# Later places for the attention splits, scores and values in the order of weight units of a one-core decoder layer

## The chip, the core and the metric

The kernel runs on one NeuronCore of a Trainium2 chip. The metric is device time in microseconds (us) of one execution of the whole layer, with all weights read from HBM. Five engines work side by side, each through its own queue in order: TensorE (PE; its weight loads are shown as PEld), VectorE (DVE), ScalarE (ACT), GpSimd (POOL) and SyncE (SP). In this kernel SP does nothing but start DMAs of weights, and POOL, once its constants are made, little but start the DMAs of the attention.

## The reference, cut to what matters

One decoder layer on x of 256 rows (positions) and 1024 columns, in float32:

```python
proj  = x @ W_in                      # q | k | v | B | C | h | gate_attn | gate_conv
y_att = attention(rope(q), rope(k), v) @ W_att      # 8 heads of 64, causal over one block of 256
y_cnv = (B * causal_dwconv3(C * h)) @ W_cnv
mix   = (sigmoid(g_att) * y_att + sigmoid(g_cnv) * y_cnv) @ W_o
x     = LayerNorm(alpha * x + mix)
u     = causal_dwconv3(x @ W_up);  f = (silu(u_gate) * u_val) @ W_down
x     = LayerNorm(alpha * x + f)
```

With 256 positions there is one key block only, so the block selection of the full reference falls away: each query attends to the earlier keys, by plain softmax. The biases of the gates are `b_gate`.

## The kernel before

**Weights and units.** TensorE multiplies in a 32-bit format that keeps fewer bits than float32. So each operand is split in two parts: the rounded value ("high") and what is left ("low"), and a product takes three passes: high by high, high by low, low by high. The host packs all weights in the order of use into 63 chunks of up to 1 MB, with two units in most chunks (134 units in all). SP fetches chunks into three buffers (`raw`). For each unit ScalarE writes the high part (`wh`, line 215) and VectorE the low part (`wl`, line 216); nine units of each have a place in SBUF. The call `ahead(u)` (line 329) puts the splits of all units up to u+4 into the queues before the matmuls of unit u.

**Stages.** Units 0 to 23 are the q, k and v columns. Units 24 to 35 are the columns of the short convolution: two units each of h, C and B for the first half of its channels, then the same for the second half. Each takes 24 matmuls (lines 312 to 314). Units 36 to 51 are the sixteen gate units, 16 matmuls each (lines 322 and 324). From unit 52 on come the output weights of attention and convolution (bank `y`), then W_o, W_up and W_down. PE's order after unit 51 isn't touched by the change.

**What sets the order.** The whole program is written out by hand in one order, from which each engine's queue follows. Between the units stands other work: `at(u, f)` notes that f is to be put into the queues behind the matmuls of unit u, and `run(u)` does so. The steps of the attention are set by a table of such numbers, with `C0` = 24. Heads go in pairs p = 0 to 3:

- `rope` and `qk_turn` (line 371), behind unit 24: q and k, which stand by rows, are transposed. VectorE turns 32 by 32 squares (line 357), eight DMAs on POOL's queue write them to DRAM (`qk_home`, line 360), and when all have landed one DMA reads them back as columns (`qk_turned`, line 363).
- `qk_hl(p)` (line 376): the two splits of the turned queries and keys of pair p, one on ScalarE and one on VectorE, into `qkT`.
- `scores(p)` (line 384): 12 matmuls into two banks `s`. `masked(p)` (line 395): on VectorE, scale, mask and row maximum. `exps(p)`: four Exp on ScalarE (line 411), of the sums also.
- `normalize(p)` and `probs_turn(p)` (lines 415 and 423): on VectorE the reciprocal, four products and the squares; then on POOL's queue four DMAs to DRAM (`p_home`), a wait for them, and one DMA back (`sm`).
- `probs_hl(p)` (line 430): the two splits of the turned probabilities into `vpt` (ScalarE, then VectorE). `attend(p)` (line 435): 6 matmuls into a bank `av`. `attend_hl(p)` (line 444): four splits into `aT`.

Beside these stand `conv1`, `conv2` and `conv3` of each half of the convolution (lines 551 to 573) behind units 28, 29 and 30 and behind units 34, 35 and 36; and for each gate unit j `gate_sum(j)` (line 595: a copy on ScalarE, a sum on VectorE), which frees the unit's bank, one of four in turn, and `gate(j)` (line 592), the Sigmoid on ScalarE.

The tile `gates` shares its memory (tag b16) with `qkT`, the tile of squares of the probabilities (tag x) with `qk_turned`.

Of the kernel before, what the change touches and what calls it, by code (L numbers as in the profile page):

```python
# [8 lines left out]
F32 = mybir.dt.float32  # L9
# [4 lines left out]
ALU = mybir.AluOpType  # L14

P = 128
S = 256
# [120 lines left out]
def layer_kernel(ctx: ExitStack, tc: tile.TileContext, x, wpack, cpack, ln1_g, ln1_b, ln2_g, ln2_b, out):  # L138
    nc = tc.nc

    cst = ctx.enter_context(tc.tile_pool(name="cst", bufs=1))
    big = ctx.enter_context(tc.tile_pool(name="big", bufs=1))
# [8 lines left out]
    def acc_bank(name):  # L151
        return psum.tile([P, 512], F32, tag="acc", name=name)

    def ps_bank(name):
        return ps_pool.tile([P, 512], F32, tag="ps", name=name)

    def scratch(shape, name, bufs=None, tag="scr"):
        return tmp.tile(shape, F32, tag=tag, name=name, bufs=bufs or 6)
# [102 lines left out]
    def bias_gate(j):  # L261
        return consts[:, 132 + j:133 + j]
# [53 lines left out]
    def unit_cols_wide(u, bank, b):  # L316


        un = units[u]
        nk = un["h"].shape[1]  # L320
        for k in range(nk):
            nc.tensor.matmul(bank, un["h"][:, k, :], b[:, k].rearrange("p a s -> p (a s)"), start=k == 0, stop=False)  # L322
        for k in range(nk):
            nc.tensor.matmul(bank[:, 0:S], un["l"][:, k, :], b[:, k, 0], start=False, stop=k == nk - 1)  # L324
# [4 lines left out]
    def ahead(u):  # L329
        for v in range(cur["u"], u + LA + 1):  # L330
            split(v)
        cur["u"] = max(cur["u"], u + LA + 1)
# [36 lines left out]
    BIG = {}  # L369
# [85 lines left out]
    def at(u, f, *a):  # L455
        after.setdefault(u, []).append((f, a))

    def run(u):
        for f, a in after.pop(u, []):
            f(*a)  # L460
# [9 lines left out]
    C0 = U[(OFF_H, 0)]  # L470
# [1 line left out]
        at(C0, rope, t)  # L472
        at(C0, qk_turn, t)
    for p in range(4):
        at(C0 + 3 + p // 2, qk_hl, p)
    for p in range(4):
        s = C0 + 4 + 3 * p
        at(s, scores, p)
        at(s + 1, masked, p)
        at(s + 2, exps, p)  # L480
        at(s + 3, normalize, p)
        at(s + 3, probs_turn, p)
        s = C0 + 9 + 4 * p
        at(s + 1, probs_hl, p)
        at(s + 3, attend, p)
        at(s + 4, attend_hl, p)


    def x_split(k):
# [85 lines left out]
    for pr in range(2):  # L575
# [3 lines left out]
        for nm, off in (("h", OFF_H), ("c", OFF_C), ("b", OFF_B)):  # L579
            bank = acc_bank(f"{nm}{pr}")  # L580
# [6 lines left out]


    GB = {}
    gates = None  # L590

    def gate(j):
        nc.scalar.activation(gates[:, j % 8, j // 8, :], GB.pop(("s", j)), AF.Sigmoid, bias=bias_gate(j))

    def gate_sum(j):
# [6 lines left out]
    for j in range(16):  # L602
        at(U[("g", 0)] + max(j, 1), gate_sum, j)
        at(U[("g", 0)] + max(j + 1, 2), gate, j)
    for j in range(16):
        u = U[("g", 0)] + j
        ahead(u)
        GB[j] = acc_bank(f"g{j}")
        unit_cols_wide(u, GB[j], xT)
        if gates is None:  # L610
            gates = big.tile([P, 8, 2, S], F32, tag="b16", name="gates")
        run(u)
    run(U[("g", 0)] + 16)
    assert not after, list(after)
# [9 lines left out]

    def mix(i, bank):
        t = scratch([P, 2, S], f"m{i}")
        nc.vector.tensor_tensor(t, gates[:, i], bank.rearrange("p (a t) -> p a t", a=2), op=ALU.mult)
        nc.vector.tensor_tensor(t[:, 0], t[:, 0], t[:, 1], op=ALU.add)
        M[i] = t[:, 0]

# [3 lines left out]
    for half in range(2):  # L634
        for e in range(2):
            ua, uc = U[("ao", half)] + e, U[("co", half)] + e
            for n in range(2):
                i = half * 4 + e * 2 + n
                if i > 1:
                    mix_hl(i - 2)  # L640
                ahead(uc + n - 1)
                bank = ps_bank(f"y{i}")
                unit_cols(uc, bank[:, 256:512], yT[:, 0], yT[:, 1], n * P)
                unit_cols(ua, bank[:, 0:256], BIG["aT"][:, 0], BIG["aT"][:, 1], n * P)
                mix(i, bank)
# [199 lines left out]
    for c in range(1, NP // 2):  # L845
        for e in range(2):
            i = 2 * c + e
# [123 lines left out]
```

## Time and profile before

| | |
|---|---|
| Time, median of 3 runs | 388.58 us (387.96 to 390.23) |
| Time of the profiled execution | 386.33 us |
| Its span, first to last instruction | 384.5 us |
| Granted TensorE clock, mean | 0.976 |
| PE busy | 360.3 us (94%) |
| DVE busy | 296.2 us (77%) |
| ACT busy | 217.5 us (57%) |

The times are the measured ones; everything else comes from one execution that the hardware profiler recorded. Its own time of 386.33 us is 1.8 us more than its span. Busy time of an engine is a sum over the whole span, and a busy PE also counts matmuls at half clock. What a stage costs is seen in the waits and in the time from one unit to the next. In a row of a timeline stand the start in us, the length in us, the engine, the line, the operation, what it writes and reads, and how many were merged (x2); in brackets stands the idle time of that engine just before, with what ended it. Matmul rows overlap, since they are pipelined: the pace is the distance from start to start.

### The profile page before, as it was taken

To read this page: it belongs to the slowest core of one execution; us is meant where nothing else is said; L and a number is where in the kernel's file an instruction comes from. 1 tells how busy PE (TensorE), PEld (TensorE's weight loads), DVE (VectorE), ACT (ScalarE), POOL (GpSimd) and SP (SyncE) were. 2 spreads that over 40 slices of the span, in tenths; PEclk is the share of its full clock that TensorE was granted. 3 is DMA by queue.
4 is the path that set the end of the run, shared out by engine and by line. 5 is a ranking of instruction groups with operands and counts; after the bars stand their busy time and mean duration, and the time that the engine had idled before them with its cause. 6 is when DMAs were issued, how large, how long until landed. Compare 5 with 4: busy or idle time off the path is not lost.

```text
span 384.5 us, 5500 instructions
## 1 busy us (share of the span) xinstructions
PE 360.3 (94%) x2082; PEld 316.0 (82%) x2082; DVE 296.2 (77%) x500; ACT 217.5 (57%) x360; POOL 24.2 (6%) x55
## 2 busy tenths in 40 slices
PE   8999946999597999999999999999999999999991
PEld 7888945997486889998888888888888888888891
DVE  4886916847858877987975989889696877999784
ACT  4767406625596875563345665767565575766400
POOL 1000400022122000010210000000000000000011
PEclk9999985999989999999999999999999999999997
DMA  7969582472664675558715176274543628562011
GB/s 257 336 237 381 175 293 83 161 248 52 242 201 149 263 281 199 187 196 340 257 73 218 47 282 232 97 300 137 221 175 154 250 86 320 218 220 110 2 55 55
DMA packets 12858, 74.88 MB, mean 195 GB/s; under 512 B 1696, under 2 KB 2336, under 8 KB 5664
## 3 DMA queue, kind: packets, MB, share of 16 engines
q1 hardware_dynamic: 10496, 67.00, 46.7%
q0 software_dynamic: 2192, 7.34, 6.3%
q8 instruction: 16, 0.26, 0.3%
q10 hardware_dynamic: 144, 0.20, 0.1%
q14 instruction: 10, 0.08, 0.1%
HBM read 70.86 MB, written 3.67 MB: 194 GB/s over the span
## 4 chain that ended last, share of the span: by engine, by line
PE 74%; DMA 8%; DVE 7%; ACT 5%; issue 2%; POOL 2%; DVEq 0%; POOLq 0%; ACTq 0%
PE pb L322 19%; PE pb L324 10%; PE d L293 5%; PE d L294 5%; PE d L295 5%; PE g L322 3%; PE q L514 3%; PE k L514 3%; PE v L514 3%; DMA sm<-p_home 2%; DMA p_home<-p_squares 2%; PE y L314 2%; PE y L313 2%; PE y L312 2%; PE o L294 2%
## 5 line engine op out<-in xcount | busy, mean ns | idle before, releaser
L216 DVE TENSOR_TENSOR wl<-raw,wh 128x1024 fp32r<-128x1024 f32 (+1 forms) x70 | 76.8, 1121 | 15.2 <-ACT wh L215 14.7
L198 DVE TENSOR_TENSOR wl<-raw,wh 128x1024 fp32r<-128x1024 f32 x58 | 70.8, 1222 | 20.6 <-ACT wh L193 20.2
L322 PE MATMUL pb<-x1T,wh 128*128 128x512 f32 x320 | 79.8, 391 | 0.0
L193 ACT ACTIVATE wh<-raw 128x1024 fp32r<-128x1024 f32 x58 | 60.8, 1052 | 25.6 <-DMA raw<-in_wpack 25.6
L215 ACT ACTIVATE wh<-raw 128x1024 fp32r<-128x1024 f32 (+1 forms) x70 | 65.7, 971 | 14.7 <-DMA raw<-in_wpack 9.1
L322 PEld LDWEIGHTS pb<-x1T,wh 128*128 128x128 f32 x320 | 58.5, 188 | 11.1
L324 PEld LDWEIGHTS pb<-x1T,wl 128*128 128x128 f32 x320 | 43.7, 190 | 3.1
L324 PE MATMUL pb<-x1T,wl 128*128 128x256 f32 x320 | 44.6, 282 | 0.0
L322 PE MATMUL g<-xT,wh 128*128 128x512 f32 x128 | 32.9, 399 | 4.0 <-DVE gs L599 3.8
L293 PE MATMUL d<-wh,f 128*128 128x512 f32 x80 | 31.3, 391 | 0.0
L294 PE MATMUL d<-wl,f 128*128 128x512 f32 x80 | 31.3, 391 | 0.0
L295 PE MATMUL d<-wh,f 128*128 128x512 f32 x80 | 31.1, 389 | 0.0
L322 PEld LDWEIGHTS g<-xT,wh 128*128 128x128 f32 x128 | 23.2, 190 | 8.6 <-issue 4.3
L734 ACT ACTIVATE fb<-pb 128x512 f32<-128x512 f32 x20 | 11.9, 594 | 16.6 <-PE pb L324 16.1
L752 DVE SCALAR_TENSOR_TENSOR fc<-fb,consts,fc 128x254 f32<-128x254 f32 x40 | 19.3, 483 | 1.4
L324 PEld LDWEIGHTS g<-xT,wl 128*128 128x128 f32 x128 | 18.3, 199 | 1.4
L750 DVE SCALAR_TENSOR_TENSOR fc<-fb,consts,fc 128x255 f32<-128x255 f32 x40 | 19.1, 478 | 0.0
L744 ACT ACTIVATE fc<-fb,consts 128x256 f32<-128x256 f32 x40 | 18.0, 498 | 1.3 <-DVE fb L738 1.3
L324 PE MATMUL g<-xT,wl 128*128 128x256 f32 x128 | 18.6, 290 | 0.0
L295 PEld LDWEIGHTS d<-wh,f 128*128 128x128 f32 x80 | 15.0, 188 | 3.2
L293 PEld LDWEIGHTS d<-wh,f 128*128 128x128 f32 x80 | 15.1, 189 | 2.7
L294 PEld LDWEIGHTS d<-wl,f 128*128 128x128 f32 x80 | 15.1, 189 | 2.6
(181 smaller groups left out, 685.9 us busy)
## 6 DMA issues: line engine op xcount, KB each, us to landing
raw<-in_wpack SPq DMA_DIRECT2D x55, 1024.0 KB, 5.2
raw<-in_wpack SPq DMA_DIRECT2D x6, 896.0 KB, 5.8
p_home<-p_squares POOLq DMA_DIRECT2D x16, 96.0 KB, 2.7
sm<-p_home POOLq DMA_DIRECT2D x4, 384.0 KB, 4.9
qk_home<-qk_squares POOLq DMA_DIRECT2D x8, 128.0 KB, 2.9
qk_turned<-qk_home POOLq DMA_DIRECT2D x1, 1024.0 KB, 5.2
xr<-in_x SPq DMA_DIRECT2D x1, 1024.0 KB, 6.8
ln<-in_ln_g POOLq DMA_DIRECT2D x2, 512.0 KB, 5.4
```

What stands on the lines that cost most here:

```text
L193: nc.scalar.activation(units[u]["h"], raw_of(u), AF.Copy)
L198: nc.vector.tensor_tensor(units[u]["l"], raw_of(u), units[u]["h"].bitcast(F32), op=ALU.subtract)
L215: nc.scalar.activation(h, src, AF.Copy)
L216: (eng or nc.vector).tensor_tensor(l, src, h.bitcast(F32), op=ALU.subtract)
L293: nc.tensor.matmul(o, ah, bh, start=start, stop=False)
L294: nc.tensor.matmul(o, ah, bl, start=False, stop=False)
L295: nc.tensor.matmul(o, al, bh, start=False, stop=stop)
L322: nc.tensor.matmul(bank, un["h"][:, k, :], b[:, k].rearrange("p a s -> p (a s)"), start=k == 0, stop=False)
L324: nc.tensor.matmul(bank[:, 0:S], un["l"][:, k, :], b[:, k, 0], start=False, stop=k == nk - 1)
L514: nc.tensor.matmul(banks[m][t], (xl if p == 2 else xh)[:, k, t * P:(t + 1) * P], wl if p == 1 else wh, start=k == 0 and p == 0, stop=k == ...
L750: nc.vector.scalar_tensor_tensor(c[:, 1:S], pb[:, a * S:a * S + S - 1], w_ffn(1, j), c[:, 1:S], op0=ALU.mult, op1=ALU.add)
L752: nc.vector.scalar_tensor_tensor(c[:, 2:S], pb[:, a * S:a * S + S - 2], w_ffn(0, j), c[:, 2:S], op0=ALU.mult, op1=ALU.add)
```

## The change

The numbers of the table become other ones, and the tile `gates` is made where the first sigmoid is issued, not behind the matmuls of the first gate unit. No operation is added or removed by the diff's lines.

```diff
     for p in range(4):
-        at(C0 + 3 + p // 2, qk_hl, p)
-    for p in range(4):
-        s = C0 + 4 + 3 * p
+        at(C0 + 6 + p, qk_hl, p)
+    for p, s in enumerate((C0 + 8, C0 + 10, C0 + 11, C0 + 12)):
         at(s, scores, p)
         at(s + 1, masked, p)
...
         at(s + 3, probs_turn, p)
-        s = C0 + 9 + 4 * p
-        at(s + 1, probs_hl, p)
-        at(s + 3, attend, p)
-        at(s + 4, attend_hl, p)
+        at(C0 + 16 + 3 * p, probs_hl, p)
+        at(C0 + 18 + 3 * p, attend, p)
+        at(C0 + 19 + 3 * p, attend_hl, p)
...
-    gates = None
 
     def gate(j):
+        if "gates" not in BIG:
+            BIG["gates"] = big.tile([P, 8, 2, S], F32, tag="b16", name="gates")
+        gates = BIG["gates"]
```

By units, for the pairs 0, 1, 2 and 3:

| step | behind unit, before | behind unit, now |
|---|---|---|
| `qk_hl` | 27, 27, 28, 28 | 30, 31, 32, 33 |
| `scores` | 28, 31, 34, 37 | 32, 34, 35, 36 |
| `masked` | 29, 32, 35, 38 | 33, 35, 36, 37 |
| `exps` | 30, 33, 36, 39 | 34, 36, 37, 38 |
| `normalize`, `probs_turn` | 31, 34, 37, 40 | 35, 37, 38, 39 |
| `probs_hl` | 34, 38, 42, 46 | 40, 43, 46, 49 |
| `attend` | 36, 40, 44, 48 | 42, 45, 48, 51 |
| `attend_hl` | 37, 41, 45, 49 | 43, 46, 49, 52 |

The first place is ScalarE's queue around the first split of the turned queries and keys. The number in `wh32` is that of the unit; the number behind the underscore only tells tiles apart. Before:

```order
L215 ACTIVATE wh31_575<-raw11_426 128x1024
L215 ACTIVATE qkT_152<-qk_turned_157 128x2x256 x2
L215 ACTIVATE wh32_610<-raw12_463 128x1024
L215 ACTIVATE qkT_152<-qk_turned_157 128x2x256 x2
L553 ACTIVATE ch0_656<-h0_462 128x512
L215 ACTIVATE wh33_661<-raw12_463 128x1024
L563 ACTIVATE ct0_696<-z0_658,consts_147 128x256 x2
```

And now:

```order
L215 ACTIVATE wh31_575<-raw11_426 128x1024
L215 ACTIVATE wh32_606<-raw12_463 128x1024
L551 ACTIVATE ch0_634<-h0_462 128x512
L215 ACTIVATE wh33_639<-raw12_463 128x1024
L561 ACTIVATE ct0_667<-z0_636,consts_147 128x256 x2
L215 ACTIVATE wh34_677<-raw13_545 128x1024
L215 ACTIVATE qkT_152<-qk_turned_157 128x2x256
L215 ACTIVATE yT_154<-ct0_667 128x512
L215 ACTIVATE wh35_710<-raw13_545 128x1024
```

The high parts of units 32, 33 and 34 and two steps of the convolution now stand ahead of the split that needs `qk_turned`; VectorE's queue moves in the same way.

The second place is VectorE's queue where the gate sums of units 36 and 37 (`gs0`, `gs1`) stand. `sm2` is the tile of pair 2, `vpt` that of the values and the split probabilities. Before:

```order
L417 RECIPROCAL st2_956<-st2_956 128x4
L421 TENSOR_SCALAR sm2_957<-sm2_957,st2_956 128x128 x2
L421 TENSOR_SCALAR sm2_957<-sm2_957,st2_956 128x256 x2
L357 STREAM_TRANSPOSE p_squares_774<-sm2_957 128x6x4x32
L599 TENSOR_TENSOR gs0_1059<-g0_976,gs0_1059 128x256
L599 TENSOR_TENSOR gs1_1062<-g1_1012,gs1_1062 128x256
L216 TENSOR_TENSOR wl42_1068<-raw17_866,wh42_1067 128x1024
L216 TENSOR_TENSOR vpt_153<-sm1_827,vpt_153 128x768
```

And now:

```order
L599 TENSOR_TENSOR gs0_1040<-g0_952,gs0_1040 128x256
L599 TENSOR_TENSOR gs1_1043<-g1_1001,gs1_1043 128x256
L216 TENSOR_TENSOR wl42_1049<-raw17_825,wh42_1048 128x1024
L417 RECIPROCAL st2_973<-st2_973 128x4
L421 TENSOR_SCALAR sm2_974<-sm2_974,st2_973 128x128 x2
L421 TENSOR_SCALAR sm2_974<-sm2_974,st2_973 128x256 x2
L357 STREAM_TRANSPOSE p_squares_911<-sm2_974 128x6x4x32
L599 TENSOR_TENSOR gs2_1087<-g2_1052,gs2_1087 128x256
L216 TENSOR_TENSOR wl43_1091<-raw17_825,wh43_1090 128x1024
L417 RECIPROCAL st3_1033<-st3_1033 128x4
```

The split of the probabilities of pair 1 (`vpt` from `sm1`) has left this place for one three units after that of pair 0, and the four turns of the probabilities follow one another at distances of two, one and one units, where they had three.

The third place is POOL's queue, whose order is the same in both, with the waits of each row in brackets. `p_home1` is the DRAM tile of pair 1. As it is now:

```order
L360 DMA p_home0_158<-p_squares_911 32x4x192 x3
L363 DMA sm0_818<-p_home0_158 128x768 [waits DMASW3_49,DMASW4_49,DMASW2_49,DMASW1_49]
L360 DMA p_home1_159<-p_squares_911 32x4x192 [waits DVE_49]
L360 DMA p_home1_159<-p_squares_911 32x4x192
L360 DMA p_home1_159<-p_squares_911 32x4x192 [waits DMASW0_49]
L360 DMA p_home1_159<-p_squares_911 32x4x192
L363 DMA sm1_919<-p_home1_159 128x768 [waits DMASW6_49,DMASW7_49,DMASW1_49,DMASW0_49]
```

The read back of pair 0 (`sm0`) waits for its four writes, and the writes of pair 1 stand behind that read. So POOL takes the turns one after another: what a turn holds up is the time from its first write to the issue of its read, while the landing of that read holds up nothing on POOL. (The DMAs take eight counters in turn; the wait for DMASW0 is for an earlier DMA on the same counter.) Nothing moved here but what lies between the turns on the other engines.

More of the change, by code (lines that the diff above doesn't have):

```diff
@@ L609, in layer_kernel @@
         unit_cols_wide(u, GB[j], xT)
-        if gates is None:
-            gates = big.tile([P, 8, 2, S], F32, tag="b16", name="gates")
         run(u)
@@ L626, in mix @@
         t = scratch([P, 2, S], f"m{i}")
-        nc.vector.tensor_tensor(t, gates[:, i], bank.rearrange("p (a t) -> p a t", a=2), op=ALU.mult)
+        nc.vector.tensor_tensor(t, BIG["gates"][:, i], bank.rearrange("p (a t) -> p a t", a=2), op=ALU.mult)
         nc.vector.tensor_tensor(t[:, 0], t[:, 0], t[:, 1], op=ALU.add)
```

## The prediction

> **What bounds the kernel now.** I read the page first, then PE's waits, then the timelines of the engines between 49 and 147 us, and the windows for the clock. The page, with PE's busy tenths and granted clock in 40 slices of 9.6 us:
>
> ```profile
> span 384.5 us, 5500 instructions
> PE   8999946999597999999999999999999999999991
> PEclk9999985999989999999999999999999999999997
> ```
>
> PE is busy from end to end but for two dips, in the sixth and seventh slice (48 to 67 us) and in the eleventh (96 to 106 us); the clock is low in the first dip and after the second. So PE bounds the kernel, and its holes are what an order can win. All of PE's waits from 37 to 150 us:
>
> ```profile
> PE s L392 <- ACT qkT L215: 8.6, 1, 8.6
> PE g L322 <- DVE gs L599: 3.8, 1, 3.8
> PE av L293 <- ACT vpt L215: 1.1, 1, 1.1
> ```
>
> They all belong to the attention or stand behind it. The timeline of PE around the largest, with starts that give the pace of each kind of work:
>
> ```profile
> 49.36 0.28 PE L312 MATMUL b<-xT,wh 128*128 128x256 f32 x1
> 49.48 0.28 PE L313 MATMUL b<-xT,wh 128*128 128x256 f32 x1
> ...
> 52.12 0.28 PE L314 MATMUL b<-xT,wl 128*128 128x256 f32 x1
> 60.99 0.47 PE L392 MATMUL s<-qkT 64*128 64x128 f32 x2 [8.59 <-ACT qkT L215]
> ```
>
> PE ends unit 28 at 52.12 + 0.28 = 52.40 and stands until 60.99, since `scores(0)` comes next and its operands aren't there. Units 29 to 31, which don't need them, stand behind it. The chain that ended last says what was late:
>
> ```profile
> 47.88 6.60 DMA qk_home<-qk_squares
> 55.06 5.22 DMA qk_turned<-qk_home
> ```
>
> The turned queries land at 55.06 + 5.22 = 60.3. The clock of the stretches, as windows (us; busy time and count of PE, PEld, DVE, ACT and POOL; PEclk; DMA share; GB/s):
>
> ```profile
> 52.40:55.40 3.00, 0.00 (x0) 0.00 (x0) 0.00 (x0) 0.00 (x0) 0.34 (x1) 1.00 1.01 422
> 55.40:65.60 10.20, 4.36 (x24) 3.95 (x25) 4.46 (x8) 4.65 (x8) 0.24 (x1) 0.50 0.31 112
> 106.60:110.10 3.50, 3.50 (x14) 3.12 (x13) 3.47 (x13) 3.47 (x6) 0.95 (x3) 0.51 0.39 95
> ```
>
> After each long hole the clock is halved for a while: a second loss of about 4.36 / 2 = 2.2 us and 3.50 / 2 = 1.7 us.
>
> **The floor.** What must PE do from 52.40 to the first matmul of `y`, if it never waits?
>
> ```profile
> 73.05 0.95 PE L392 MATMUL s<-qkT 64*128 64x128 f32 x12
> 73.93 0.39 PE L312 MATMUL c<-xT,wh 128*128 128x256 f32 x1
> ...
> 136.71 0.40 PE L293 MATMUL av<-vpt 128*128 128x512 f32 x1
> 137.76 0.63 PE L322 MATMUL g<-xT,wh 128*128 128x512 f32 x2
> ...
> 146.13 0.28 PE L312 MATMUL y<-yT,wh 128*128 128x256 f32 x1
> ```
> ```profile
> 143.50 1.84 PE g L322 x8
> 145.34 0.95 PE g L324 x8
> ```
>
> A unit of the convolution is 24 matmuls at 0.12 us (49.48 - 49.36) = 2.88; seven are left, 20.2. A gate unit is 1.84 + 0.95 = 2.79; sixteen, 44.6. Scores take 73.93 - 73.05 = 0.88, four times, 3.5; the values 137.76 - 136.71 = 1.05, four times, 4.2. Together 72.5: `y` could begin at 124.9 where it begins at 146.1. So 21.2 us is all that this change can win. Behind 146.1 PE's order is the old one, and I count that part at nothing either way: units 52 and up have their splits as far ahead as before.
>
> **Part 1, the first splits stand three units later.** The landing at 60.3 is not made earlier: `rope` and the turn keep their place. But PE now goes on with units 29 to 32, and needs `qkT` only behind unit 32, at 52.4 + 4 x 2.88 = 63.9. ScalarE and VectorE still wait for the landing, with the splits of unit 34 done; PE has work for 52.4 + 6 x 2.88 = 69.7, so the hole of 8.6 and its half clock go, if the landing isn't late. It may be: the two queues now split units 32 and 33 before they wait, which frees a `raw` buffer at about 52.4, and SP fetches a chunk of 1 MB just when the turned queries are read. The DMA engines were full until 55.4 (share 1.01, 422 GB/s). A chunk that takes its turn there costs between nothing and 1 MB / 422 GB/s = 2.5 us; I take 1.5, since the share after 55.4 is only 0.31. The Trainium skill, page "DMA: Bandwidth & Descriptors", section "Issuing engines are not separate DMA queues", says that DMAs of SP and POOL run on the same 16 engines and interleave; by it alone the delay would be near the upper end, and the sum 1 us longer. No run here shows that overlap yet.
>
> **Part 2, VectorE's queue becomes dense.** The steps of four pairs now stand between units 32 and 39, beside the weights, the second half of the convolution and the first gate sums. VectorE begins at the landing, and PE's next hard demand on it is `attend(0)` behind unit 42, which needs the `vpt` split behind unit 40. Rows of VectorE's timeline, each step from its start to the next one's:
>
> ```profile
> 60.97 1.29 DVE L216 TENSOR_TENSOR qkT<-qk_turned,qkT 128x512 fp32r<-128x512 f32 x2 [11.63 <-ACT qkT L215]
> ...
> 64.79 0.68 DVE L556 TENSOR_TENSOR z<-c,ch 128x512 f32<-128x512 f32 x1
> ...
> 66.53 0.28 DVE L400 CUSTOM_DVE_ANT_0 sm<-s,mask 128x128 f32<-128x128 f32 x1
> ...
> 67.83 1.92 DVE L566 SCALAR_TENSOR_TENSOR ct<-z,consts,ct 128x256 f32<-128x256 f32 x4
> 69.66 1.22 DVE L216 TENSOR_TENSOR wl<-raw,wh 128x1024 fp32r<-128x1024 f32 x1
> 70.80 0.68 DVE L572 TENSOR_TENSOR ct<-b,ct 128x512 f32<-128x512 f32 x1
> 72.18 0.69 DVE L216 TENSOR_TENSOR yT<-ct,yT 128x512 fp32r<-128x512 f32 x1 [0.70 <-ACT yT L215]
> ...
> 74.27 0.17 DVE L417 RECIPROCAL st<-st 128x4 f32<-128x4 f32 x1
> ...
> 76.42 1.19 DVE L216 TENSOR_TENSOR wl<-raw,wh 128x1024 fp32r<-128x1024 f32 x1
> ```
> ```profile
> L599 DVE TENSOR_TENSOR gs<-g,gs 128x256 f32<-128x256 f32 x16 | 6.6, 419 | 6.5 <-ACT gs L598 6.4
> L216 DVE TENSOR_TENSOR vpt<-sm,vpt 128x768 fp32r<-128x768 f32 x4 | 3.8, 953 | 5.6 <-ACT vpt L215 5.6
> ```
>
> In that stretch stand ten low parts (units 35 to 44) at 70.80 - 69.66 = 1.14, 11.4; four `qkT` splits at 1.29 / 2, 2.6; `z` 0.68; four masks at 67.83 - 66.53 = 1.30, 5.2; the taps 69.66 - 67.83 = 1.83; twice the last step of the convolution at 0.68 + 0.69, 2.7; four times reciprocal, products and squares at 76.42 - 74.27 = 2.15, 8.6; five gate sums at 0.42, 2.1; one `vpt` split, 0.95. Sum 36.0 us, so from 60.97 VectorE is there at 97.0 at the earliest. PE without a wait reaches `attend(0)` at 52.4 + 7 x 2.88 + 4 x 0.88 + 7 x 2.79 = 95.6. The two run level, and each late handoff makes PE wait. Those are: two waits for `yT` of 0.70 (row 72.18), and ScalarE's Exp and Sigmoid with their table loads in between; I take 2.5 us (nothing to 6). With 1.5 from part 1, `attend(0)` is at 101.0.
>
> Before that, unit 40 needs the bank of unit 36, freed by a gate sum that stands behind the third pair's softmax; this is the place of the old wait of 3.8 us, and it will again be short by about 2. It is part of the same lag, not a further term.
>
> **Part 3, ScalarE's table.** All Exp now stand ahead of all Sigmoids; before, a Sigmoid stood between the third and the fourth pair's Exp.
>
> ```profile
> L411 ACT ACT_TABLE_LOAD x2 | 2.6, 1283 | 0.0
> L593 ACT ACT_TABLE_LOAD x2 | 2.6, 1283 | 0.9 <-DVE gs L599 0.9
> ```
>
> Two of the four loads of 1283 ns go. ScalarE is the less loaded engine, so I count this at nothing by itself; it keeps the 2.5 us of handoffs from being more. That `gates` is made later moves no operation: the first Sigmoid stood behind the last scores before and does now.
>
> **Part 4, the round trips of the probabilities.** On POOL:
>
> ```profile
> 76.80 2.19 POOL L360 DMA_DIRECT2D p_home<-p_squares  x4 [21.16 <-DVE p_squares L357]
> 81.60 0.57 POOL L363 DMA_DIRECT2D sm<-p_home  x1 [2.61 <-DMA p_home<-p_squares]
> ...
> 118.64 2.19 POOL L360 DMA_DIRECT2D p_home<-p_squares  x4 [8.28 <-DVE p_squares L357]
> 126.36 0.57 POOL L363 DMA_DIRECT2D sm<-p_home  x1 [5.53 <-DMA p_home<-p_squares]
> ```
> ```profile
> 81.60 6.22 DMA sm<-p_home
> ```
>
> A turn holds POOL for 81.60 + 0.57 - 76.80 = 5.4 to 126.36 + 0.57 - 118.64 = 8.3 us, and its read lands about 6 later. Now four turns queue up: the first is ready when VectorE has done 13.9 us of the list above (2.6 + 1.4 + 5 x 1.14 + 1.3 + 0.7 + 2.15), with the 4 us of lateness at about 78. At 8.3 each the reads are issued by 86, 95, 103 and 111 and land by 92, 101, 109 and 117. They are wanted by ScalarE behind units 40, 43, 46 and 49, that is at about 98, 107, 115 and 124. Hidden, with 6 us to spare; if that cover goes, each us beyond it is one us of PE.
>
> **The sum.** After `attend(0)` at 101.0 come four times 1.05 and nine gate units: 101.0 + 4.2 + 25.1 = 130.3. PE then has waited 130.3 - 124.9 = 5.4 us in two or three holes of 1 to 3 us. The hole of 3.8 us before cost a stretch at half clock, 1.7 us, that of 1.1 none; I take one such stretch: 132.0. The Trainium skill, page "TensorE: Matmul & The Clock Gate", section "Part 1: The HAM clock gate", has the clock halved after an idle window of about 3.4 us, the windows running free. The half stretch from 106.6 to 110.1 agrees; by that rule holes of 2 us would mostly cost nothing, and `y` would begin at 130.3.
>
> So `y` begins 146.1 - 132.0 = 14.1 us earlier. The profiled execution of 386.33 us becomes 372.2; it lies 2.3 under the median of 388.58, from which I subtract the same: **374.5 us**.
>
> **The rivals.** *No engine is late* (17 to 21 us won, 367.4 to 371.6): VectorE's 97.0 is within 1.4 us of PE's 95.6, and if landing and handoffs cost little, only the floor is left. Against it speak the many handoffs between two dense queues. 0.17.
>
> *The turned data come late* (2 to 9.5 us won, 379 to 386.6): the DMA engines, which now also carry weights without a pause, stretch the landing at 60.3 by 5 to 12 us, and every us goes to `attend(0)`. For it speaks the share of 1.01 at 52.4; against it that only one freed chunk can stand in the way. 0.10.
>
> *The wait only moves* (within 0.5%, 1.9 us, which is what a measurement can tell from no change): landing later by 12 us or more, or VectorE's handoffs costing as much. 0.04.
>
> *Slower: the four round trips queue up on POOL.* They lie close now, under a VectorE that never pauses. If a turn holds POOL for x, the fourth lands at 78 + 4x + 6, and `y` follows 132.0 - 124 = 8 us later: 92 + 4x. It decides from x = 13.5, where that is 146; at x = 16 `y` begins at 156, and the time is 398.5. Against it: no turn above took over 8.3, and the four writes of the first were issued in 2.19 us, in part under a running `wl` (row 76.42). The Trainium skill, page "SBUF — State Buffer", section "SBUF: two separate sides", has a rule against this change: while VectorE runs operations that take both port pairs, GpSimd can't write the descriptors of its DMAs. The 2.19 us row doesn't show it. 0.04.
>
> **How the numbers follow.** My forecast, 9.5 to 17 us won, has 0.65. The range takes in the middle of the first rival and the milder half of the second: 369.0 to 381.0. Faster by over 0.5%: 0.65 + 0.17 + 0.10 = 0.92, less 0.01 for what borders on no change: 0.91; within 0.5% 0.05; slower 0.04.
>
> **What would show it.** Right: no wait of PE for `qkT` over 2.5 us, clock near 1.0 from 55 to 65 us; `qk_turned` landed by 63; PE's holes then at unit 40 for `gs` and at `attend(0)` for `vpt`, together 3 to 7 us; two table loads fewer; the four `sm` landed ahead of ScalarE's splits; `y` at 128 to 136. Wrong: ScalarE waiting for `sm`, `qk_turned` after 66, VectorE with gaps between 61 and 100 while PE waits, or a stage behind `y` that takes longer than its 238.4 us (384.5 - 146.1) now.

## The result and the profile after

The changed kernel takes 373.68 us (median of 4 runs, 373.11 to 374.72) beside 388.27 us for the kernel before on the same chip (387.46 to 390.23): a ratio of 0.962, with a 95% interval of 0.9576 to 0.9664. The prediction was 374.5 us, faster. The profiled execution of the changed kernel took 373.11 us, with a mean granted clock of 0.988 (0.976 before).

The page of the changed kernel, with PE's busy tenths and granted clock in slices of 9.3 us:

```profile
span 371.3 us, 5482 instructions
...
PE   8999999989989999999999999999999999999991
...
PEclk9999999998999999999999999999999999999997
```

The deep dips of the sixth, seventh and eleventh slice are gone. Two shallow ones are left, in the ninth and the twelfth, and the clock falls once, to 8 tenths. The span is 384.5 - 371.3 = 13.2 us shorter. Two rows of PE's timeline, the scores of the last pair and the first matmul of `y`:

```profile
80.98 0.58 PE L392 MATMUL s<-qkT 64*128 64x128 f32 x3 [1.82 <-DVE st L400]
...
132.96 0.28 PE L312 MATMUL y<-yT,wh 128*128 128x256 f32 x1
```

`y` begins at 132.96, where it began at 146.13: 13.2 us again, so all of it was won ahead of `y`. PE's waits of the changed kernel from 37 to 150 us (us in total, times, longest):

```profile
PE av L294 <- DVE vpt L216: 1.9, 1, 1.9
PE s L392 <- DVE st L400: 1.8, 1, 1.8
PE g L322 <- DVE gs L599: 0.6, 1, 0.6
PE s L392 <- DVE qkT L216: 0.4, 1, 0.4
PE s L392 <- ACT qkT L215: 0.2, 1, 0.2
```

The wait of 8.6 us for the turned queries has become two waits of 0.6 together. What is left, 4.9 us, is nearly all for VectorE. The windows of the changed kernel: the stretch that ran at half clock before, the one that does now, and all that lies from `y` on.

```profile
55.40:65.60 10.20, 9.60 (x83) 9.13 (x82) 2.52 (x3) 1.89 (x3) 0.58 (x1) 1.00 0.59 232
82.75:86.15 3.40, 3.40 (x12) 2.82 (x11) 3.37 (x12) 0.63 (x4) 0.57 (x1) 0.50 0.26 65
132.95:371.30 238.35, 230.47 (x1290) 201.56 (x1288) 195.69 (x306) 130.41 (x205) 6.09 (x8) 0.99 0.48 177
```

From 55 to 65 us the clock is now full. One stretch of 3.4 us at 0.50 is left, behind the wait of 1.8 us at the last scores. From `y` on it takes 238.35 us; 384.5 - 146.13 = 238.4 before. So all is won ahead of it. Windows from the first matmul of unit 24 (`h`) to the first of `y` part it, of the kernel before:

```profile
37.85:146.13 108.28, 92.96 (x617) 84.26 (x616) 74.81 (x148) 63.48 (x120) 16.18 (x29) 0.94 0.57 197
```

And of the changed kernel:

```profile
37.54:132.96 95.42, 90.44 (x618) 82.29 (x617) 75.21 (x147) 61.08 (x119) 16.23 (x29) 0.98 0.65 226
```

PE stood for 108.28 - 92.96 = 15.3 us and now for 95.42 - 90.44 = 5.0: 10.3 won. Its busy time fell by 92.96 - 90.44 = 2.5, since less of the same work runs at half clock. Together that is the 108.28 - 95.42 = 12.9 us of the distance; the other 0.3 lie ahead of `h` (37.85 to 37.54).

The chain of the changed kernel, where the turned data come from:

```profile
48.12 6.99 DMA qk_home<-qk_squares
...
55.70 7.41 DMA qk_turned<-qk_home
63.13 0.64 ACT qkT L215
```

They land at 55.70 + 7.41 = 63.1, 2.8 us later than before. VectorE's timeline from there: the first and last row of the list that the prediction made, its longest idle time, and the gate sums of units 36 and 37:

```profile
63.79 0.69 DVE L216 TENSOR_TENSOR qkT<-qk_turned,qkT 128x512 fp32r<-128x512 f32 x1 [6.36 <-ACT qkT L215]
...
75.77 0.69 DVE L554 TENSOR_TENSOR z<-c,ch 128x512 f32<-128x512 f32 x1 [1.26 <-ACT ch L551]
...
92.47 0.75 DVE L599 TENSOR_TENSOR gs<-g,gs 128x256 f32<-128x256 f32 x2
...
102.76 0.95 DVE L216 TENSOR_TENSOR vpt<-sm,vpt 128x768 fp32r<-128x768 f32 x1
```

The list runs from 63.79 to 102.76 + 0.95 = 103.71, and it is its last row that PE waits for with the first values (`vpt`, 1.9 us above). The first gate sum begins 92.47 - 63.79 = 28.68 us behind the first split; this distance comes back below. POOL's first and third turn of the probabilities, and ScalarE's table loads and splits of them between 60 and 150 us:

```profile
80.38 2.19 POOL L360 DMA_DIRECT2D p_home<-p_squares  x4 [24.11 <-DVE p_squares L357]
84.97 0.57 POOL L363 DMA_DIRECT2D sm<-p_home  x1 [2.40 <-DMA p_home<-p_squares]
...
97.98 2.26 POOL L360 DMA_DIRECT2D p_home<-p_squares  x4
107.46 0.57 POOL L363 DMA_DIRECT2D sm<-p_home  x1 [7.22 <-DMA p_home<-p_squares]
```
```profile
L215 ACT ACTIVATE vpt<-sm 128x768 fp32r<-128x768 f32 x4 | 3.4, 844 | 0.1
...
L411 ACT ACT_TABLE_LOAD x1 | 1.3, 1283 | 0.0
L593 ACT ACT_TABLE_LOAD x1 | 1.3, 1283 | 0.0
```

A turn holds POOL for 84.97 + 0.57 - 80.38 = 5.2 us at the start and for 107.46 + 0.57 - 97.98 = 10.1 us in the third pair, more than the 8.3 seen before. ScalarE waits 0.1 us in all ahead of its four splits of `vpt`: the turns are hidden. The loads are two instead of four.

### The profile page after: what moved, and what is told of

It is laid out like the page before. It is cut to its first block, busy times and chain, and to the rows that moved or that the text cites. A ratio compares the mean times of both kernels' runs of the same rounds, so it can differ in the third digit from the quotient of the medians.

```text
span 371.3 us, 5482 instructions
## 1 busy us (share of the span) xinstructions
PE 357.4 (96%) x2082; PEld 314.2 (85%) x2082; DVE 296.2 (80%) x500; ACT 214.2 (58%) x358; POOL 24.2 (7%) x55
## 4 chain that ended last, share of the span: by engine, by line
PE 70%; DVE 11%; DMA 9%; ACT 5%; issue 2%; POOL 1%; SPq 1%; DVEq 0%; ACTq 0%; POOLq 0%
PE pb L322 20%; PE pb L324 10%; PE d L293 5%; PE d L294 5%; PE d L295 5%; DMA raw<-in_wpack 5%; PE g L322 4%; DVE wl L216 4%; ACT wh L215 3%; PE g L324 2%; PE y L312 2%; PE y L314 2%; PE y L313 2%; DMA qk_turned<-qk_home 2%; PE o L293 2%
## 5 line engine op out<-in xcount | busy, mean ns | idle before, releaser
L732 ACT ACTIVATE fb<-pb 128x512 f32<-128x512 f32 x20 | 11.8, 592 | 13.3 <-PE pb L324 12.7
```

## The experiments

**The theory** behind the prediction: the hole at the turned queries goes since PE has other units to do there, and what is left of the win is set by VectorE's list from the landing to the first values. **The rivals** tested with it: that the later splits, the later values or the fewer table loads bring the win, and not the later scores; and that something other than VectorE's list (landing, round trips, clock) holds the rest. Ratios are to the kernel before in rounds on one chip, with their 95% intervals; the changed kernel's is 0.962 (0.9576 to 0.9664). The chips differ from experiment to experiment, and the kernel before took 386.79 to 388.27 us on them, so a time of one experiment compares with that of another only to about 1.5 us. The traces of two kernels start a little apart, so stages are compared by the distance from `h` to `y` in the two windows above: 108.28 before, 95.42 after.

### The splits at their old place

```diff
-        at(C0 + 6 + p, qk_hl, p)
+        at(C0 + 3 + p // 2, qk_hl, p)
```

> The changed kernel, with the splits of the turned queries and keys back behind units 27 and 28, and all else at its new place. My theory (the order lets ScalarE and VectorE work on while the turn is under way, and VectorE's queue from the landing to the first values sets the time): PE runs to the end of unit 31 (61 us) and then waits some 2 to 3 us for the weights of unit 32, whose splits now stand behind the landing; VectorE has the low parts of units 32 to 34, z and the taps still to do after the landing, about 6 us more, and the landing is earlier by up to 2.5 us since no chunk is fetched beside it. So the first values 2 to 4 us later than in the changed kernel, y at 135 to 137 us, time 376 to 378 us. Rival (only the place of the scores matters, since it alone made PE wait): y at 133 us, time 373.7 us as in the changed kernel.

Measured: 380.38 us, 0.9835 (0.9776 to 0.9895). By the distance from `h` to `y`, 139.81 - 38.89 = 100.92, that is 5.5 us more than the changed kernel (6.7 by the times), more than the 2 to 4 of the theory; the rival's 373.7 is out. The waits and one window of this kernel:

```profile
ACT qkT L215 <- DMA qk_turned<-qk_home: 19.0, 1, 19.0
...
PE c L312 <- ACT ch L551: 5.5, 1, 5.5
```
```profile
65.75:72.60 6.85, 5.06 (x23) 5.07 (x24) 6.61 (x12) 4.54 (x8) 0.00 (x0) 0.50 0.22 44
```

ScalarE stands for 19.0 us at the split for which the data aren't there. What PE then lacks first isn't, as expected, the weights of unit 32. It is a bank: conv1's copy (line 551), which reads the `h` bank, stands on ScalarE behind that split, and unit 32 needs a bank. PE stands for 5.5 us and then runs 6.85 us at half clock. So the splits must stand later as well; a wait at the head of a queue holds back all that stands behind it.

### The values nearer, and the values later

```diff
-        at(C0 + 16 + 3 * p, probs_hl, p)
-        at(C0 + 18 + 3 * p, attend, p)
-        at(C0 + 19 + 3 * p, attend_hl, p)
+        at(C0 + (14, 17, 19, 21)[p], probs_hl, p)
+        at(C0 + (16, 19, 21, 23)[p], attend, p)
+        at(C0 + (16, 19, 21, 23)[p] + 1, attend_hl, p)
```

> The changed kernel, with the splits of the turned probabilities behind units 38, 41, 43 and 45 (3, 4, 5 and 6 units behind their turns, as far as they stood before the change) and the values two units behind each. My theory (the turns follow one another on POOL, some 10 us each, so the later places of the values are needed): pairs 0 and 1 arrive in time, the reads of pairs 2 and 3 land at about 113 and 122 us and are wanted at about 108 and 116; ScalarE and VectorE stand still for them with weights behind, PE waits 3 to 8 us in all, time 376 to 381 us. Rival (the places of the values are free, only those of the scores count): within 1 us of 373.7.

Measured: 373.05 us, 0.9638 (0.9605 to 0.9671). The theory fell here: one turn was late, by 1.3 us on ScalarE, and PE never waited 3 to 8 us for the values (0.2 in all). The wait moved to unit 40. Two lines of this kernel's waits:

```profile
PE g L322 <- DVE gs L599: 2.2, 1, 2.2
...
ACT vpt L215 <- DMA sm<-p_home: 1.3, 1, 1.3
```

In the second kernel the numbers are (18, 21, 23, 25) for `probs_hl` and (20, 23, 25, 27) for `attend`:

> The changed kernel, with the splits of the turned probabilities behind units 42, 45, 47 and 49 and the values behind 44, 47, 49 and 51. My theory (VectorE is behind by about two units at the first values and catches up after): PE's wait of 1.95 us at the first values goes, the gate units that run instead wait at most 0.5 us for their banks, y at 131 us, time 371.5 to 372.5 us. Rival (VectorE's backlog passes on to the banks of the gate units, so the wait only moves): no change, 373.7 us.

Measured: 373.16 us, 0.9645 (0.9603 to 0.9688), no change that the intervals can tell, as the rival had it. Its wait at unit 40, and the window behind it:

```profile
PE g L322 <- DVE gs L599: 2.2, 1, 2.2
```
```profile
94.60:98.05 3.45, 3.45 (x14) 3.08 (x13) 2.81 (x8) 3.42 (x8) 0.00 (x0) 0.51 0.25 65
```

The wait of 1.9 us for the first values is gone, the one for `gs` has grown from 0.6 to 2.2, and the stretch at half clock (3.45 / 2 = 1.7 us) now lies behind it. From the nearer to the later of these places the time is the same: the values don't carry the gain.

### A chunk of weights held back at the landing

```diff
 def ahead(u):
-        for v in range(cur["u"], u + LA + 1):
+        la = 3 if u == C0 + 5 else 2 if u == C0 + 6 else LA
+        for v in range(cur["u"], u + la + 1):
             split(v)
-        cur["u"] = max(cur["u"], u + LA + 1)
+        cur["u"] = max(cur["u"], u + la + 1)
```

> The changed kernel, with the splits of units 33 and 34 put behind the first split of the turned queries, so that no buffer comes free and no chunk of weights is fetched while the turn is read back. Theory: in the changed kernel the read took 7.4 us, in the old one 5.2, because of that chunk; so here the landing is at 60 to 61.5 us, where it was at 63.1. VectorE's list after the landing grows by two low parts, 2.3 us, so the first gate sums end within 1 us of where they did (93.2), and the time stays within 1 us of the changed kernel's. Rival (the landing itself sets the time): y and the end 2 us earlier. Rival (the longer read has another cause): landing at 63 and the time 2 us longer.

Measured: 374.63 us, 0.9688 (0.9646 to 0.973). The read of `qk_turned` in its trace, and two new waits:

```profile
DMA to landing us min/median/max: 5.6/5.6/5.6
```
```profile
PE c L314 <- DVE wl L216: 0.8, 1, 0.8
...
PE c L312 <- ACT wh L215: 0.5, 1, 0.5
```

The read took 5.6 us beside 7.4 in the changed kernel and 5.2 before. While it ran the DMA engines moved 200 GB/s x 5.6 us = 1.1 MB, in the changed kernel 302 x 7.41 = 2.2 MB: there the chunk of weights flows at the same time. How much of the longer read is the chunk's is less sure, since the kernel with the splits at their old place moved only 186 x 6.59 = 1.2 MB in its read, and that took 6.6 us. Nothing was won: the weights held back came late themselves (0.8 + 0.5 us), and VectorE's first gate sum stood 93.52 - 62.58 = 30.9 us behind its first split, in place of 28.7, which is the two low parts that now stand behind the landing. From `h` the first split came 1.7 us earlier (62.58 - 38.05 = 24.5 beside 63.79 - 37.54 = 26.2) and `y` 0.5 later (134.00 - 38.05 = 95.95): the earlier landing and the longer list just add up.

### The softmax of the first pair one unit later

```diff
-        at(s + 3, normalize, p)
-        at(s + 3, probs_turn, p)
+        at(s + 3 + (p == 0), normalize, p)
+        at(s + 3 + (p == 0), probs_turn, p)
```

> The changed kernel, with the softmax end and the turn of the first pair one unit later, behind unit 36, so that the mask of the second pair comes ahead of them and frees the banks of the last scores 2 us earlier. Theory (the sum of PE's waits is set by how far VectorE's queue has come at the gate sums and the first values, not by each wait): the wait of 1.83 us for the last scores goes, the one for the first gate sum, 0.62 us, grows by about as much, and the time stays within 1 us of the changed kernel's (a stretch at half clock may come or go, 1.7 us). Rival (each wait stands for itself): the time 1.8 us less.

Measured: 374.01 us, 0.9649 (0.9615 to 0.9684). The wait of 1.8 us at the last scores is gone, and the one for `gs` has grown from 0.6 to 3.5. Rows of VectorE's timeline, of its waits and of its windows:

```profile
65.62 0.69 DVE L216 TENSOR_TENSOR qkT<-qk_turned,qkT 128x512 fp32r<-128x512 f32 x1 [7.01 <-ACT qkT L215]
...
94.30 0.75 DVE L599 TENSOR_TENSOR gs<-g,gs 128x256 f32<-128x256 f32 x2
```
```profile
PE g L322 <- DVE gs L599: 3.5, 1, 3.5
```
```profile
94.10:101.00 6.90, 6.23 (x19) 5.30 (x20) 5.69 (x15) 6.45 (x16) 2.38 (x5) 0.51 0.47 184
```

94.30 - 65.62 = 28.68 us, the same as in the changed kernel, although the steps between stand in another order. (It is 28.67 to 28.68 in the two kernels with the values moved and in the next one, too.) So the waits of PE are shares of one lag: the step that is moved out of one wait is paid in the next. All of PE's waits from 37 to 150 us sum to 4.9 us here, and to 5.0 in the changed kernel. `y` begins 135.40 - 39.16 = 96.24 us behind `h`, 0.8 later than there, with 6.9 us at half clock in place of 3.4.

### The last Exp behind the first gates

```diff
-        at(s + 2, exps, p)
+        at(s + 2 + (p == 3), exps, p)
```

> The changed kernel, with the Exp of the last pair one unit later, behind the first two Sigmoids, so that ScalarE loads its tables four times there, as before the change, and not twice: 2.6 us more on ScalarE. Theory (VectorE's queue is the bound and ScalarE only hands over to it): the last softmax end and the third and fourth gate sum come 1 to 3 us later, y 0.5 to 2.5 us later, time 0.5 to 2.5 us more than the changed kernel's 373.7. Rival (ScalarE has room, loads are hidden): within 0.5 us.

Measured: 373.96 us, 0.9646 (0.9615 to 0.9676): the theory fell, and the two loads that this brings back cost nothing that can be measured. One window over the whole stretch:

```profile
60.00:132.80 72.80, 67.02 (x434) 59.08 (x433) 57.81 (x121) 53.86 (x107) 10.98 (x20) 1.00 0.59 209
```

This execution has no half clock at all, and its `y` begins at 132.80, 94.84 us behind `h`, 0.6 less than in the changed kernel with its 1.7 us of lost clock. Its first values wait for a `vpt` split that ends at 102.59 + 0.95 = 103.54, 39.6 us behind its first split at 63.94. So the loads don't make VectorE's list longer (39.9 us in the changed kernel), and the half clock at 83 us of the changed kernel costs little: every wait of VectorE in its list there is for ScalarE, none for PE, so PE would else wait longer for the same row of VectorE.

### The products of the softmax on ScalarE

```diff
-                nc.vector.tensor_scalar(pr[:, j, PCOL[t]], pr[:, j, PCOL[t]], st[:, 12 + i:13 + i], None, op0=ALU.mult)
+                nc.scalar.activation(pr[:, j, PCOL[t]], pr[:, j, PCOL[t]], AF.Copy, scale=st[:, 12 + i:13 + i])
```

> The changed kernel, with the four products of each softmax end on ScalarE in place of VectorE: 4 x 1.0 us off VectorE's queue, some 1.5 to 1.8 us more per pair on ScalarE and two more handovers per pair. Theory (VectorE's queue from the landing to the first gate sums and the first values sets what is left of PE's waits): two of the four ends lie ahead of the gate sum that unit 40 waits for, so that comes 1 to 2 us earlier, the wait of 1.95 us for the first values shrinks to under 1 us, time 1 to 3 us less than the changed kernel's. Rival (the handovers cost what the queue gains): within 1 us, or longer.

Measured: 381.45 us, 0.9839 (0.9806 to 0.9871). The theory of a lighter VectorE fell. The waits:

```profile
DVE p_squares L357 <- ACT sm L421: 6.5, 4, 1.6
...
ACT sm L421 <- DVE st L417: 5.8, 4, 1.4
...
PE g L322 <- DVE gs L599: 3.5, 2, 2.7
PE av L293 <- ACT vpt L215: 2.7, 1, 2.7
```

The products take VectorE 1.01 us a pair, 4 in all. Moved, each pair is handed to ScalarE and back, and VectorE stands 6.5 us for the return alone. Work that is taken from the limiting engine, but that this engine then waits for, doesn't shorten its list.

### The scores spread over the gate units

The old distance of three units between the pairs, but from unit 32 on, so that the hole at the turned queries stays away:

```diff
-    for p, s in enumerate((C0 + 8, C0 + 10, C0 + 11, C0 + 12)):
+    for p, s in enumerate((C0 + 8, C0 + 11, C0 + 14, C0 + 17)):
```

> The changed kernel, with the scores behind units 32, 35, 38 and 41, three apart as before the change (mask, Exp and turn one, two and three units behind each); splits and values of the probabilities stay at the new places. My theory (density of VectorE's queue ahead of the first values is what is left of PE's waits): VectorE has one mask and two softmax ends, 5.6 us, less to do ahead of the first values, so the waits of 1.8, 0.6 and 1.95 us go, at the price of four more table loads on ScalarE; y at 127 to 130 us, time 368 to 371 us. Rival (the close place of the scores is what brought the gain, since Exp and Sigmoid then don't alternate): slower than the changed kernel by 2 us or more.

Measured: 387.64 us, 0.9983 (0.9948 to 1.0019): all of the gain is gone, and the theory, which saw a lighter VectorE, fell clearly. Waits, a row each of ScalarE's and of PE's timeline, and the loads:

```profile
PE av L293 <- ACT vpt L215: 5.7, 3, 2.4
...
ACT vpt L215 <- DMA sm<-p_home: 4.2, 1, 4.2
...
PE g L322 <- DVE gs L599: 3.4, 3, 1.8
...
PE av L294 <- DVE vpt L216: 1.7, 4, 0.6
```
```profile
96.88 0.91 ACT L593 ACTIVATE gates<-gs,consts 128x256 f32<-128x256 f32 x2 [4.81 <-PE s L392]
```
```profile
143.70 0.50 PE L293 MATMUL av<-vpt 128*128 128x512 f32 x1 [1.73 <-ACT vpt L215]
```
```profile
L411 ACT ACT_TABLE_LOAD x3 | 3.8, 1283 | 0.1
L593 ACT ACT_TABLE_LOAD x3 | 3.8, 1283 | 0.0
```

ScalarE has become the late engine. Its first Sigmoid waits 4.81 us for scores, since the gates write over the memory of `qkT`; Exp and Sigmoid take turns, with six loads; and the last pair's turn, begun later, is late: ScalarE waits 4.2 us for it, and PE at 143.70 for ScalarE, right ahead of `y` (145.63). Two kernels take away one of the first two each. In the first the gates are Exp, too, so this kernel leaves out the Sigmoid:

```diff
-        nc.scalar.activation(gates[:, j % 8, j // 8, :], GB.pop(("s", j)), AF.Sigmoid, bias=bias_gate(j))
+        nc.scalar.activation(gates[:, j % 8, j // 8, :], GB.pop(("s", j)), AF.Exp, bias=bias_gate(j))
```

> The kernel with the scores spread over units 32, 35, 38 and 41, with Exp in place of Sigmoid for the gates: the gates are then no gates (that part of the function is changed), but ScalarE does the same count of steps of the same size and never changes its table there. In the spread kernel with Sigmoid, y began at 145.6 us and the time was that of the kernel before. Theory (it was lost to six table loads, 1.28 us each, that stand in the chain copy, gate sum, bank): without them PE's waits in the gate units fall from some 12 to under 5 us, y at 131 to 136 us, time 371 to 377 us. Rival (not the loads but the Exp, masks and softmax ends themselves among the gate units, and the splits of the values right behind them): y at 141 us or later, time over 382 us.

Measured: 382.55 us, 0.9836 (0.9781 to 0.9891). Five of the six loads of that stretch are gone (5 x 1.28 = 6.4 us), and `y` begins 140.38 - 39.65 = 100.73 us behind `h`, where the spread kernel has 145.63 - 38.37 = 107.26: 6.5 less. That is less than the theory's 371 to 377 us would need, so the loads are a part and not the whole. The wait for the memory is still there:

```profile
ACT gates L593 <- PE s L392: 6.1, 1, 6.1
```

In the second the first eight gates have the memory of another tile, that of the rows of q and k (tag rows), so that none of them meets `qkT`:

```diff
-        if "gates" not in BIG:
-            BIG["gates"] = big.tile([P, 8, 2, S], F32, tag="b16", name="gates")
-        gates = BIG["gates"]
-        nc.scalar.activation(gates[:, j % 8, j // 8, :], GB.pop(("s", j)), AF.Sigmoid, bias=bias_gate(j))
+        if j == 0:
+            BIG["gates", 0] = big.tile([P, 8, S], F32, tag="rows", name="gates")
+        if j == 8:
+            BIG["gates", 1] = big.tile([P, 8, 2, S], F32, tag="b16", name="gatesc")[:, :, 0]
+        nc.scalar.activation(BIG["gates", j // 8][:, j % 8], GB.pop(("s", j)), AF.Sigmoid, bias=bias_gate(j))
```

> The spread kernel (scores behind units 32, 35, 38 and 41) with memory for the first eight gates that the turned queries and keys don't use (that of the q and k rows, which are done), and the other eight where all were. Theory (the spread kernel's first Sigmoid stood 4.8 us on ScalarE, 6.1 in the one with Exp, until the scores of the third pair had been read from the shared memory, with the gate sums behind it): that wait goes, PE's wait of 1.75 us for the gate sum of unit 38 too, and y comes 2 to 5 us earlier than at 145.6, time 382 to 386 us; the table loads' share of some 5 us stays. Rival (the wait was slack on ScalarE): time as in the spread kernel, 387.6 us.

Measured: 380.74 us, 0.983 (0.9796 to 0.9864); `y` begins 139.60 - 38.72 = 100.88 us behind `h`, 6.4 less and more than the 2 to 5 of the theory; the rival is out. The longest of PE's waits that remain:

```profile
PE av L293 <- ACT vpt L215: 4.0, 2, 2.4
```

So the spread costs 107.26 - 95.42 = 11.8 us of distance, and 1.7 more behind `y` (240.07 us to the end in place of 238.35), which neither edit wins back. Loads and memory are each shown to cost, but the two gains don't simply add up. In both kernels PE's busy time from `h` to `y` falls too, from 95.10 us to 91.56 and 91.79, since less of it runs at half clock. These some 3.4 us stand in either gain and can be won only once. With both edits about 6.5 + 6.4 - 3.4 = 9.5 us would go, as an estimate; the late turn of the last pair, for which ScalarE still waits 3.7 and 2.2 us in the two kernels, is the third cost. No kernel had both edits.

### The low parts of two units on POOL

```diff
-            split(v)
+            split(v, nc.gpsimd if v in (C0 + 11, C0 + 12) else None)
```

> The changed kernel, with the low parts of units 35 and 36 computed on POOL, which stands idle from 56 to 80 us, in place of VectorE: 2 x 1.14 us less in VectorE's list between the landing and the first values. Theory (that list sets PE's waits): the masks, gate sums and values come 2 us earlier, PE's waits of 1.8, 0.6 and 1.95 us fall to under 2.5 in all, time 1 to 3.5 us less than the changed kernel's 373.7, if POOL takes no more than 5 us for each (no trace here shows such a step; unit 35 is needed at 72 and unit 36 at 76 us, and their high parts are there at 67 and 68). Rival (POOL is slower than that, or VectorE's steps beside it get longer): time as before or more, with PE waiting for the low part of unit 35 or 36.

Measured: 376.17 us, 0.9707 (0.9668 to 0.9745): slower than the changed kernel, and the theory fell. POOL's timeline, and VectorE's beside it:

```profile
67.62 5.23 POOL L216 TENSOR_TENSOR wl<-raw,wh 128x1024 fp32r<-128x1024 f32 x2 [11.05 <-ACT wh L215]
```
```profile
68.09 5.31 DVE L216 TENSOR_TENSOR qkT<-qk_turned,qkT 128x512 fp32r<-128x512 f32 x2 [0.78 <-ACT qkT L215]
```

POOL takes 5.23 us for two low parts. In that time VectorE does two splits of 0.69 each, and they last 5.31. VectorE was to save 2 x 1.14 us and loses 5.31 - 2 x 0.69 = 3.9; its first gate sum stands 95.56 - 64.63 = 30.9 us behind its first split, in place of 28.7. With the later values as well (the numbers of the second kernel above):

> Both: the low parts of units 35 and 36 on POOL, and the splits of the turned probabilities and the values one to two units later as in the kernel with the values behind 44, 47, 49 and 51. Theory (VectorE's list sets the waits, and a first wait for gate sums under 1.6 us starts no stretch at half clock): no wait of PE over 1 us from 65 us on, y at 129 to 131 us, time 369.5 to 371.5 us. Rival (POOL's steps cost what they bring): 373 us or more.

Measured: 374.41 us, 0.9657 (0.9624 to 0.9691). The theory fell here too: PE waits 3.8 us for the last scores, whose masks stand behind the two long splits. Whether a hole under 1.6 us never starts a stretch at half clock, this kernel can't tell, since its one stretch follows that long wait. No kernel was found that beats the changed one by more than a measurement can tell.

## Why the prediction was right, point by point

**Sign, size and mechanism held**: 13.2 us of the profile against 14.1 predicted, 373.68 against 374.5. How near the number came is in part luck. Two terms of the sum were off, and they offset each other. And the profiled execution of the kernel before lies 388.27 - 386.33 = 1.9 us under the median, that of the changed one 0.6, so the medians differ by 14.6 us where the profiles differ by 13.2.

**What bounds the kernel.** The three lines given as all of PE's waits from 37 to 150 us are three of seven: the others, 0.9, 0.5, 0.3 and 0.2 us, are waits for VectorE. The forecast doesn't rest on them, since its floor is counted from PE's work.

**Part 1.** The hole of 8.6 us and its half clock went. The prediction has PE covered until 69.7, which is a step too far: `scores(0)` stands behind unit 32 in PE's queue, so the cover ended at the 63.9 that the text has just before. The two waits for `qkT`, 0.6 us together, are what the landing at 63.1 cost there. The landing was mis-sized: a delay of 1.5 us was taken, between nothing and 2.5, and the read alone took 7.41 - 5.22 = 2.2 more, the writes ahead of it end 0.6 later: 63.1 in place of 61.8, just past the 63 of the text. The kernel that holds the chunk of weights back (5.6 us) points to the chunk as the cause; that one read without a chunk took 6.6 leaves its exact share open. The rule of the Trainium skill that the prediction cited here ("DMA: Bandwidth & Descriptors", section "Issuing engines are not separate DMA queues"), by which the delay would be near the upper end, was nearer than the value taken.

**Part 2.** VectorE's steps were nearly right, its handoffs too small. The list took 39.9 us against 36.0 + 2.5 = 38.5. Its idle times in the brackets between 63.79 and 103.71 sum to 4.6 us: the two named waits for `yT`, 0.59 and 0.52 behind the last Exp and the Sigmoid's table load, short ones for `wh`, and the largest, 1.26 at `z`, for a copy that stands on ScalarE behind the first pair's Exp. The steps took 39.9 - 4.6 = 35.3, in part since four gate sums, and not five, stand ahead of the `vpt` split. Together with the landing (63.79 in place of 62.5) the first values came at 103.7 instead of 101.0.

That this list sets `y`, three more kernels bear out, in which VectorE's first gate sum comes 30.9 to 34.8 us behind its first split, and not 28.7. From that gate sum to `y` pass 132.96 - 92.47 = 40.49 us in the changed kernel, 139.81 - 99.31 = 40.50 with the old splits, 134.00 - 93.52 = 40.48 with the chunk held back and 136.15 - 95.56 = 40.59 with POOL's low parts: what the list loses, `y` loses. (Where values or softmax steps are moved as well it is 38.8 to 41.1; with the products on ScalarE, where PE waits again behind that sum, 47.5.)

**The half clock** was one stretch of 1.7 us, as predicted, but not where: it lay at 83 us, ahead of the first values, and not behind them. There it is under the lag of VectorE and adds little, as the kernel without any half clock suggests. So the sum's last term of 1.7 falls away and the one before it is 2.7 too small: 132.0 + 2.7 - 1.7 = 133.0, and measured is 132.96.

**The holes.** 5.0 us in place of 5.4. They were named at unit 40 and at the first values. The prediction missed the one at the last scores: `scores(3)` needs the banks of pair 1, whose mask stands on VectorE behind the softmax of pair 0. It is one more face of the same lag, and took from the wait at unit 40 what it cost, as the kernel with that softmax moved shows.

**Parts 3 and 4.** Two loads went and brought nothing, as counted; the kernel with four has the same time. Four turns queued up on POOL, and the third held it for 10.1 us, above the 8.3 allowed but short of the 13.5 from which it would have decided. The rule of the Trainium skill against this change ("SBUF — State Buffer", section "SBUF: two separate sides", the descriptors blocked by VectorE) was not borne out: four writes are issued in 2.19 to 2.26 us under a dense VectorE, as before. Whether any of VectorE's steps here takes both port pairs, no row shows.

**What the prediction didn't see** is why the scores must stand close together ahead of the gate units. It took this for a cost (VectorE gets dense) and not for a part of the gain. The spread kernel has no hole at the turned queries and yet the old time. So the changed order needs two things beside the later first scores: the splits go later with them (left out, 5.5 us of the distance are lost), and the scores stand close together, all read before the first Sigmoid writes over `qkT` (left out, 11.8 us of the distance, and the whole gain by the time). That every Exp stands ahead of every Sigmoid isn't needed: with the last pair's behind the first two, nothing was lost.

**What stays open.** What each of memory, loads and the late last turn costs the spread when the others are gone; what an earlier landing is worth without a longer list. That `gates` is made later was not tried alone: with it made at the old place the queues of all five engines read the same, row by row, so no time is put down to it.

## What to carry to other kernels

A wait ahead of the limiting engine is removed by giving it other work, but count what the other in-order queues hold back behind the same wait: here a copy that frees a bank. When two dense engines run level, the holes of one are a single lag of the other: find the list that sets it and time it from its first to its last row, since moving one step only moves the hole. And steps that read memory which the next stage writes over belong ahead of that stage, even where they crowd an engine; a change of function table counts only where ScalarE is the late engine (two loads more cost nothing in one kernel, five fewer won 6.5 us in another).

## What the runs showed of the hardware

**Short holes halve the clock, sometimes.** The hole of 1.8 us at 79 us of the changed kernel was followed by 3.4 us at 0.50; one of 2.2 in the kernel with later values by 3.45; one of 3.5 by 6.9; the kernel with Exp between had holes of 1.8 and 2.2 and no half clock in its profiled execution. The stretches are about one or two times 3.4 us. The Trainium skill, page "TensorE: Matmul & The Clock Gate", section "Part 1: The HAM clock gate", has free-running windows of about 3.4 us, which agrees; its idle window of that length before the clock falls doesn't agree with the hole of 1.8 us: in the 3.41 us ahead of the fall at 82.75, PE was busy for 1.77.

**POOL's arithmetic stops VectorE's.** Two VectorE splits of 0.69 us stood for 5.31 us beside two subtractions on POOL of 2.6 each. The Trainium skill, page "SBUF — State Buffer", section "SBUF: two separate sides", has the two engines lock each other out where an operation of VectorE reads two operands from SBUF and one of GpSimd reads SBUF as well; the rows agree.
